# Dilated v projection: its staging for DRAM in the raw weights' ring instead of the score rows' ring

## The chip, the cores and the metric

The kernel runs on one core of one Trainium2 chip. The metric is the device time of one execution in microseconds; the runs shown of the kernel before took 1883.52 us in the median (1883.05 to 1884.08, three runs).

## What is computed

One layer of a decoder trunk over 1024 tokens of width 1024, all in float32. The part that matters here is the dilated window attention, one of four token mixers:

```python
DIL_PATTERNS = ((128, 1), (512, 4), (2048, 16))      # (window, dilation) of three groups
qb, kb, vb = (a.reshape(bsz, seq, N_DIL_GROUPS, N_DIL_HEADS, HEAD_DIM) for a in (qb, kb, vb))
...
for g, (window, dil) in enumerate(DIL_PATTERNS):
    idx = t_idx[:, None] - dil * jnp.arange(window // dil + 1)[None, :]
    kg, vg = jnp.take(k[:, :, g], idx, axis=1), jnp.take(v[:, :, g], idx, axis=1)
    s = jnp.einsum('bqhd,bqnhd->bhqn', q_blk[:, :, g], kg) * HEAD_DIM ** -0.5
    s = s - slopes[g][:, None, None] * dists                 # then softmax over n
    outs.append(jnp.einsum('bhqn,bqnhd->bqhd', p, vg))
```

q, k and v of every mixer are columns of one product, RMSNorm(x) @ w_in. After the mixers come gated branch projections, an output projection and a squared-ReLU MLP.

## The kernel before

Every float32 product is made of float32r parts: an operand is split into a high part and a low rest, and three matmuls on TensorE stand for one (`mm3`, L148 to L155: high times high, high times low, low times high). Weights come through three rings of four buffers each (`wpiece`, L117): a piece of 256 KB is loaded by SP's queue into `wr` (L125), GpSimd makes its high part `wh` (L132) and its low part `wl` (L133), and with that `wr` is free again. The buffers of `wr` have other tenants too: the copies `gs` of gate logits on their way to DRAM (L492 to L495) use the same ring.

The mixers run as twelve units, two (`pr` 0 and 1, two heads each) for each of six groups. A unit has a projection part, `p_`, and an attention part, `a_`; the projection of the next unit is written ahead of the end of this one's attention, so that its matmuls (`lin`, `linv`, in three PSUM banks of the pool `ps_lin`) fill TensorE while attention waits for VectorE and ScalarE. For a dilated group the order of work is: v of the group (`proj_v`), q and k of its first pair (`proj_pair`, whose `lin_T` takes 128 columns of weights in two pieces), attention of the first pair, q and k of the second, attention of the second.

`proj_v` makes v in four blocks of two token tiles (48 matmuls of 256 columns each, `linv`). For dilation 4 and 8 (the reference's 16, in 8 residue classes) tokens have to be regrouped by residue, which goes through DRAM: ScalarE copies each half of the bank to a staging tile `vs` (high part, L158), VectorE writes the low rest beside it (L162), ScalarE's queue stores the half to `v_d` (L390), and when all is stored, SP's queue loads it back in the new order into `v` (L399): 8 loads for dilation 4, 16 for dilation 8. Staging in the kernel before takes one tile of the ring `s` for both halves. That ring has five buffers (`NS`, L56) and holds the score rows of attention (`s2` in `attend_dil`) and the rows of the differential mixer's norm (`ysq`, `sp`, `r0`, L671 to L694).

What stands in which order on an engine is set by a list scheduler: it takes instructions by priority (the order in the code, with the evacuations put ahead by `EVAC_LEAD`) as their inputs and buffers come free in its own model of time. A ring with no free buffer thus moves instructions to later places in the queues; on the chip each engine and each queue goes through its own list in order.

Of the kernel before, what the change touches and what calls it, by code (L numbers as in the profile page):

```python
# [12 lines left out]
F32 = mybir.dt.float32  # L13
F32R = mybir.dt.float32r
# [8 lines left out]
P = 128  # L23
T = 1024
# [35 lines left out]
NWR, NWH, NS, NPT, NQK = 4, 4, 5, 6, 12  # L60
# [4 lines left out]
def kernel(  # L65
# [27 lines left out]
    wp = ctx.enter_context(tc.tile_pool(name="wp", bufs=1))  # L93
# [19 lines left out]
    def nm(s):  # L113
        uid[0] += 1
        return f"{s}_{uid[0]}"
# [33 lines left out]
    def mm3(ps, pairs):  # L149

        n = len(pairs)
        for i, ((ah, al), (bh, bl)) in enumerate(pairs):
            nc.tensor.matmul(ps, ah, bh, start=(i == 0), stop=False, skip_group_check=True)  # L153
            nc.tensor.matmul(ps, ah, bl, start=False, stop=False, skip_group_check=True)  # L154
            nc.tensor.matmul(ps, al, bh, start=False, stop=(i == n - 1), skip_group_check=True)  # L155

    def evac_hi(o, i, scale=1.0):
        nc.scalar.activation(o, i, AF.Copy, scale=scale)  # L158

    def evac_lo(o, i, hi, scale=1.0):  # L160
        if scale == 1.0:
            nc.vector.tensor_sub(o, i, hi.bitcast(F32))  # L162
        else:
            nc.vector.scalar_tensor_tensor(o, i, scale, hi.bitcast(F32), op0=ALU.mult, op1=ALU.subtract)
# [49 lines left out]
    with ExitStack() as actx:  # L214
# [87 lines left out]
        def w_next(off, n):  # L302
            assert plan[0] == (off, n), (plan[0], off, n)
            plan.pop(0)
            return held.pop() if held else wcols(w_in, off, n)
# [55 lines left out]
        def proj_v(voff, dil, fl=None):  # L361

            n = 260 if fl is not None else 256
            ws = w_next(voff, n)
            vt = [ap_.tile([P, NT, 2, P], F32R, tag="v", bufs=3, name=nm("v")) for _ in range(2)]
            v_d = [dram.tile([T, 4 * 64], F32, name=nm("v_d")) for _ in range(2)] if dil > 1 else None
            per = 1 if fl is not None else 2
            for b0 in range(0, NT, per):
                ps = ps_lin.tile([P, 512], F32, tag="lin", name=nm("linv"))
                for j in range(per):  # L370
                    ts_ = slice((b0 + j) * P, (b0 + j + 1) * P)
                    pairs = [((hTh[:, k, ts_], hTl[:, k, ts_]), ws[k]) for k in range(NK)]
                    if fl is not None:
                        mm3(ps[:, :n], pairs)
                    else:

                        mm3(ps.rearrange("p (a b c) -> p a b c", a=2, b=2)[:, :, j], pairs)
                if dil > 1:
                    vs = s_tile("vs")[:, :T].bitcast(F32R).rearrange("p (a b d) -> p a b d", a=2, d=P)
                with tc.high_priority(offset=EVAC_LEAD):  # L380
                    for p in range(2):
                        i = ps[:, p * per * P:(p + 1) * per * P].rearrange("p (a d) -> p a d", d=64)
                        if dil > 1:
                            o = vs[:, p]
                        else:
                            o = vt[p].rearrange("p b h d -> p (b h) d")[:, 2 * b0:2 * (b0 + per)]
                        evac_hi(o[:, :, 0:64], i)
                        evac_lo(o[:, :, 64:128], i, o[:, :, 0:64])
                        if dil > 1:
                            nc.scalar.dma_start(  # L390
                                v_d[p][b0 * P:(b0 + per) * P, :].rearrange("(b p) c -> p b c", p=P),
                                o.rearrange("p (b h) d -> p b (h d)", b=per).bitcast(F32))
                    if fl is not None:
                        nc.vector.tensor_add(fl[:, :, b0], ps[:, 256:260], bf_row)
            if dil > 1:
                m = T // dil // P
                for p in range(2):
                    for r in range(dil):
                        nc.sync.dma_start(  # L399
                            vt[p][:, r * m:(r + 1) * m].rearrange("p b h d -> p b (h d)").bitcast(F32),  # L400
                            v_d[p].rearrange("(b p r) c -> r p b c", r=dil, p=P)[r])
            return vt

        def s_tile(n):
            return ap_.tile([P, T + 8], F32, tag="s", bufs=NS, name=nm(n))
# [398 lines left out]
        def unit_diff(pr):  # L804
            def p_():
                if pr == 0:
                    state["v"] = proj_v(DIF_V, 1)
                v = state["v"]
                qs, ks = proj_diff(pr)
                return lambda: attend_diff(pr, qs, ks, v[pr])  # L810
            return p_

        def unit_dil(g, pr):
            def p_():
                if pr == 0:
                    state["v"] = proj_v(DIL_V + g * 256, DILATION[g])
                    state["mnl"] = small.tile([P, 2, 4, NT], F32, tag="mnl", bufs=2, name=nm("mnl"))
                v, mnl = state["v"], state["mnl"]
                q, k, kl = proj_pair(DIL_Q + g * 256 + pr * P, DIL_K + g * 256 + pr * P, -0.125, DILATION[g])

                def a_():
                    attend_dil(g, pr, q, k, kl, v[pr], mnl)
                    if pr == 1:
                        dil_stats(g, mnl)
                return a_
            return p_

        def unit_fox(pr):
            def p_():
                if pr == 0:  # L830
                    fl = small.tile([P, 4, NT], F32, name="fl")
                    state["v"] = proj_v(FOX_V, 1, fl)
                    state["cq"] = fox_cum(fl)
                v, cq = state["v"], state["cq"]
                q, k, kl = proj_pair(FOX_Q + pr * P, FOX_K + pr * P, -0.125, 1)
                return lambda: attend_fox(pr, q, k, kl, v[pr], cq)
            return p_
# [602 lines left out]
```

## Time and profile before

| | |
|---|---|
| median of the runs shown | 1883.52 us |
| the profiled execution | 1883.11 us, its span 1881.4 us |
| TensorE busy | 1834.4 us, 98% of the span |
| VectorE, ScalarE, GpSimd busy | 1083.7, 846.2, 766.5 us |
| `vs` evacuations of dilation 4 | from 432.2 us on |
| `vs` evacuations of dilation 8 | last at 549.7 us |

Times in the trace count from the start of the span; the profiled execution has 1.7 us outside it. Matmuls overlap in the pipeline, so that a row's own length is more than its share: what a matmul costs is the distance from one start to the next.

### The profile page before, as it was taken

To read this page: it belongs to the slowest core of one execution; us is meant where nothing else is said; L and a number is where in the kernel's file an instruction comes from. 1 tells how busy PE (TensorE), PEld (TensorE's weight loads), DVE (VectorE), ACT (ScalarE), POOL (GpSimd) and SP (SyncE) were. 2 spreads that over 40 slices of the span, in tenths; PEclk is the share of its full clock that TensorE was granted. 3 is DMA by queue.
4 is the path that set the end of the run, shared out by engine and by line. 5 is a ranking of instruction groups with operands and counts; after the bars stand their busy time and mean duration, and the time that the engine had idled before them with its cause. 6 is when DMAs were issued, how large, how long until landed. Compare 5 with 4: busy or idle time off the path is not lost.

```text
span 1881.4 us, 27436 instructions
## 1 busy us (share of the span) xinstructions
PE 1834.4 (98%) x9683; PEld 1554.3 (83%) x9683; DVE 1083.7 (58%) x1907; ACT 846.2 (45%) x1731; POOL 766.5 (41%) x715
## 2 busy tenths in 40 slices
PE   7999999999999999998999999989999999999998
PEld 7888888889888889887788879978888888888886
DVE  5144464544454555677653596595444445759677
ACT  4133334454464544454342454554554545444344
POOL 5434244423222243532323471077564641418165
PEclk9999999999989999999999999999999999999999
DMA  4634213234243221126314764525444448675455
GB/s 147 160 103 118 68 51 90 62 102 157 68 139 92 63 79 57 54 63 188 98 59 149 250 225 158 174 90 183 158 141 160 136 146 305 220 229 198 123 179 185
DMA packets 214137, 255.39 MB, mean 136 GB/s; under 512 B 17392, under 2 KB 136560, under 8 KB 214000
## 3 DMA queue, kind: packets, MB, share of 16 engines
q1 hardware_dynamic: 174880, 176.39, 30.8%
q10 hardware_dynamic: 39120, 77.25, 12.2%
q8 instruction: 76, 1.25, 0.3%
q14 instruction: 61, 0.50, 0.1%
HBM read 174.25 MB, written 65.70 MB: 128 GB/s over the span
## 4 chain that ended last, share of the span: by engine, by line
PE 88%; DVE 5%; DMA 2%; POOL 2%; ACT 1%; issue 1%; SPq 1%; ACTq 0%; POOLq 0%; DVEq 0%
PE pu L1145 5%; PE pu L1146 5%; PE pu L1143 5%; PE lg L153 5%; PE pd L1334 5%; PE pd L1332 5%; PE lg L154 5%; PE pd L1333 5%; PE lg L155 5%; PE lin L153 5%; PE lin L154 5%; PE lin L155 5%; PE pt L430 3%; PE linv L154 2%; PE linv L153 2%; PE linv L155 2%
## 5 line engine op out<-in xcount | busy, mean ns | idle before, releaser
L132 POOL TENSOR_SCALAR wh<-wr 128x512 fp32r<-128x512 f32 (+1 forms) x156 | 106.4, 683 | 438.6 <-PE linv L155 116.9
L133 POOL TENSOR_TENSOR wl<-wr,wh 128x512 fp32r<-128x512 f32 (+1 forms) x160 | 220.1, 1379 | 9.5
L153 PE MATMUL lg<-hTh,wh 128*128 128x512 f32 x464 | 185.7, 400 | 0.0
L154 PE MATMUL lg<-hTl,wh 128*128 128x512 f32 x464 | 185.6, 400 | 0.0
L155 PE MATMUL lg<-hTh,wl 128*128 128x512 f32 x464 | 184.9, 399 | 0.0
L1333 PE MATMUL pd<-wl,sh 128*128 128x512 f32 x444 | 174.3, 393 | 0.6 <-DVE wl L1054 0.6
L1334 PE MATMUL pd<-wh,sl 128*128 128x512 f32 x444 | 173.9, 394 | 0.0
L1332 PE MATMUL pd<-wh,sh 128*128 128x512 f32 x444 | 171.9, 394 | 0.0
L153 PE MATMUL lin<-hTh,wh 128*128 128x512 f32 x384 | 153.1, 399 | 0.0
L154 PE MATMUL lin<-hTl,wh 128*128 128x512 f32 x384 | 153.0, 399 | 0.0
L155 PE MATMUL lin<-hTh,wl 128*128 128x512 f32 x384 | 151.9, 398 | 0.0
L1054 DVE TENSOR_TENSOR sl<-mg,sh 128x512 fp32r<-128x512 f32 x111 | 107.0, 967 | 69.9 <-ACT sh L1053 69.7
L1053 ACT CAST sh<-mg 128x512 fp32r<-128x512 f32 x111 | 68.6, 620 | 142.5 <-PE pd L1333 126.8
L435 DVE TENSOR_TENSOR ptl<-pt,pth 128x512 fp32r<-128x512 f32 (+2 forms) x168 | 99.3, 605 | 55.5 <-ACT pth L434 54.2
L434 ACT CAST pth<-pt 128x512 fp32r<-128x512 f32 (+2 forms) x168 | 84.7, 524 | 95.4 <-PE pt L430 91.1
L153 PE MATMUL linv<-wh,hTh 128*128 128x256 f32 (+1 forms) x384 | 112.0, 293 | 2.2 <-ACT hTh L195 0.9
L154 PE MATMUL linv<-wl,hTh 128*128 128x256 f32 (+1 forms) x384 | 112.0, 292 | 0.0
L155 PE MATMUL linv<-wh,hTl 128*128 128x256 f32 (+1 forms) x384 | 111.9, 292 | 0.0
L153 PEld LDWEIGHTS lg<-hTh,wh 128*128 128x128 f32 x464 | 87.9, 189 | 17.9 <-DVE dst L162 0.2
L155 PEld LDWEIGHTS lg<-hTh,wl 128*128 128x128 f32 x464 | 87.6, 189 | 17.3
L154 PEld LDWEIGHTS lg<-hTl,wh 128*128 128x128 f32 x464 | 87.8, 189 | 17.1
L1333 PEld LDWEIGHTS pd<-wl,sh 128*128 128x128 f32 x444 | 83.4, 188 | 20.6 <-DVE wl L1054 1.0
(360 smaller groups left out, 5044.8 us busy)
## 6 DMA issues: line engine op xcount, KB each, us to landing
wr<-in_w_in_dram SPq DMA_DIRECT2D x132, 256.0 KB
br<-in_w_down_dram SPq DMA_DIRECT2D x96, 256.0 KB
mg<-sa_s SPq DMA_DIRECT2D x64, 256.0 KB
gl<-gs ACTq DMA_DIRECT2D x58, 256.0 KB
sg<-gl SPq DMA_DIRECT2D x58, 256.0 KB
mg<-sa_a SPq DMA_DIRECT2D x48, 256.0 KB
wr<-in_w_out_dram SPq DMA_DIRECT2D x36, 256.0 KB
dm<-dst ACTq DMA_DIRECT2D x64, 128.0 KB
```

The costliest lines, as they stand in the source:

```text
L132: nc.gpsimd.tensor_scalar(hi, raw, 1.0, 1.0, op0=ALU.mult, op1=ALU.mult)
L133: (eng or nc.gpsimd).tensor_sub(lo, raw, hi.bitcast(F32))
L153: nc.tensor.matmul(ps, ah, bh, start=(i == 0), stop=False, skip_group_check=True)
L154: nc.tensor.matmul(ps, ah, bl, start=False, stop=False, skip_group_check=True)
L155: nc.tensor.matmul(ps, al, bh, start=False, stop=(i == n - 1), skip_group_check=True)
L435: nc.vector.tensor_sub(lo[:, :n], ps[:, :n], hi[:, :n].bitcast(F32))
L1054: nc.vector.tensor_sub(o[1], i, o[0].bitcast(F32))
L1143: nc.tensor.matmul(ps[:, cs], w_, bh[:, k, cs], start=first and k == 0, stop=False, skip_group_check=True)
L1145: nc.tensor.matmul(ps[:, cs], w_, bl[:, k, cs], start=False, stop=False, skip_group_check=True)
L1332: nc.tensor.matmul(ps, sh[0][:, ts_], w[0], start=start and j == 0, stop=False, skip_group_check=True)
L1333: nc.tensor.matmul(ps, sh[0][:, ts_], w[1], start=False, stop=False, skip_group_check=True)
L1334: nc.tensor.matmul(ps, sh[1][:, ts_], w[0], start=False, stop=last and j == NPAIR - 1, skip_group_check=True)
```

## The change

The staging tile of both halves, one buffer of the ring `s`, is replaced by two buffers of the ring `wr`, one for each half:

```diff
                 if dil > 1:
-                    vs = s_tile("vs")[:, :T].bitcast(F32R).rearrange("p (a b d) -> p a b d", a=2, d=P)
+
+                    vs = [wp.tile([P, 520], F32, tag="wr", bufs=NWR, name=nm("vs"))[:, :512].bitcast(F32R)
+                          .rearrange("p (b d) -> p b d", d=P) for _ in range(2)]
...
                         if dil > 1:
-                            o = vs[:, p]
+                            o = vs[p]
```

The instructions are the same; those on which buffers depend come in another order, in the stretch from the v projection of dilation 4 to that of dilation 8. Lines behind the change are higher by two.

SP's queue at the v projection of dilation 4 (`wr` with 128x4x128 are pieces of q and k weights, `v` from `v_d` the regrouped loads). Before:

```order
L125 DMA wr_4669<-in_w_in_dram 128x4x128
L125 DMA wr_4675<-in_w_in_dram 128x4x128
L125 DMA wr_4745<-in_w_in_dram 128x4x128
L125 DMA wr_4751<-in_w_in_dram 128x4x128
L680 DMA ysq_4817<-yd_89 128x512
L125 DMA wr_5046<-in_w_in_dram 128x4x128
L672 DMA ysq_4832<-yd_89 128x512
L125 DMA wr_5052<-in_w_in_dram 128x4x128
L399 DMA v_4430<-v_d_4432 128x2x256 x4
```

After:

```order
L682 DMA ysq_4821<-yd_89 128x512
L125 DMA wr_4673<-in_w_in_dram 128x4x128
L125 DMA wr_4679<-in_w_in_dram 128x4x128
L674 DMA ysq_4836<-yd_89 128x512
L401 DMA v_4430<-v_d_4432 128x2x256 x4
L401 DMA v_4431<-v_d_4433 128x2x256 x4
L125 DMA wr_4749<-in_w_in_dram 128x4x128
L125 DMA wr_4755<-in_w_in_dram 128x4x128
```

The two pieces of q weights (4669 and 4675 before, 4673 and 4679 now) still stand ahead of the v loads, but in buffers that staging tiles of the third block hold before them; the two pieces of k weights (4745 and 4751 before, 4749 and 4755 now) have moved behind all eight v loads.

TensorE at the end of the third block of the v projection of dilation 8 (`sc`, `pt` and `o` are scores, transposes and outputs of the attention of dilation 4, second pair). Before:

```order
L155 MATMUL linv_5566<-wh_5445,hTl 128x2x128
L411 MATMUL sc_5243<-kA_5116,qA_5044 128x128
L412 MATMUL sc_5243<-klA_5118,qA_5044 128x128
L411 MATMUL sc_5248<-kA_5116,qA_5044 128x256
L412 MATMUL sc_5248<-klA_5118,qA_5044 128x256
L430 MATMUL pt_5230<-ident,s_5219 128x128 x3
L411 MATMUL sc_5270<-kA_5116,qA_5044 128x128
```

After:

```order
L155 MATMUL linv_5572<-wh_5449,hTl 128x2x128
L153 MATMUL linv_5629<-wh_5431,hTh 128x2x128
L154 MATMUL linv_5629<-wl_5432,hTh 128x2x128
L155 MATMUL linv_5629<-wh_5431,hTl 128x2x128
L153 MATMUL linv_5629<-wh_5431,hTh 128x2x128
L154 MATMUL linv_5629<-wl_5432,hTh 128x2x128
```

Before, 75 matmuls of attention follow the third block alone and the fourth block (5622) comes behind them; now the fourth block (5629) follows at once, and attention comes between its matmuls and behind it, with the q projection of dilation 8 in its later part.

SP's queue at the v projection of dilation 8. Before, the k weights (5773 and 5779) are loaded long ahead:

```order
L125 DMA wr_5697<-in_w_in_dram 128x4x128
L125 DMA wr_5703<-in_w_in_dram 128x4x128
L125 DMA wr_5773<-in_w_in_dram 128x4x128
L125 DMA wr_5779<-in_w_in_dram 128x4x128
L680 DMA ysq_5194<-yd_89 128x512
```

After:

```order
L125 DMA wr_5705<-in_w_in_dram 128x4x128
L125 DMA wr_5711<-in_w_in_dram 128x4x128
L401 DMA v_5454<-v_d_5456 128x256 x8
L401 DMA v_5455<-v_d_5457 128x256 x8
L125 DMA wr_5781<-in_w_in_dram 128x4x128
```

The k weights (5781) stand behind all sixteen v loads now.

## Rows read from the trace of the kernel before

**Rows 1.** The page: busy time of each engine, its share of the span, and its instructions.

```profile
PE 1834.4 (98%) x9683; PEld 1554.3 (83%) x9683; DVE 1083.7 (58%) x1907; ACT 846.2 (45%) x1731; POOL 766.5 (41%) x715
```

**Rows 2.** Busy time of each engine by stretch (us), then TensorE's granted clock, the DMA engines' busy share and GB/s.

```profile
526.87:533.70 6.83, 6.64 (x32) 6.62 (x33) 4.66 (x21) 4.85 (x18) 0.00 (x0) 0.50 0.10 38
...
540.52:543.93 3.41, 3.41 (x19) 3.41 (x18) 1.41 (x4) 1.04 (x3) 0.00 (x0) 0.50 0.88 291
...
523.77:540.18 16.41, 12.29 (x71) 11.12 (x70) 13.61 (x50) 12.80 (x44) 0.00 (x0) 0.79 0.09 32
...
450.94:462.40 11.46, 11.46 (x50) 9.24 (x50) 6.13 (x8) 6.54 (x9) 10.33 (x10) 1.00 0.80 238
```

**Rows 3.** TensorE in order of time around the fourth v block of dilation 8: start, length, operation; in brackets the idle time before it and what ended that.

```profile
509.79 0.28 PE L155 MATMUL linv<-wh,hTl 128*128 128x256 f32 x1
...
523.49 0.28 PE L155 MATMUL linv<-wh,hTl 128*128 128x256 f32 x1
524.84 0.33 PE L411 MATMUL sc<-kA,qA 128*128 128x128 f32 x1 [1.06 <-DVE mnl L725]
...
537.09 0.28 PE L412 MATMUL sc<-klB,qB 128*128 128x256 f32 x1
539.22 0.35 PE L439 MATMUL o<-pth,v 128*128 128x256 f32 x1 [1.85 <-DVE y L454]
...
549.28 0.28 PE L441 MATMUL o<-ptl,v 128*128 128x256 f32 x1
...
550.13 0.45 PE L682 MATMUL rms<-sp,ones_blk 128*128 128x512 f32 x1
...
550.65 0.42 PE L155 MATMUL lin<-hTh,wl 128*128 128x512 f32 x1
...
557.64 0.40 PE L154 MATMUL lin<-hTl,wh 128*128 128x512 f32 x1
...
560.90 0.39 PE L153 MATMUL lin<-hTh,wh 128*128 128x512 f32 x1
```

**Rows 4.** All instructions on the tile `vs`: shortest, median and longest (ns), first and last start (us).

```profile
L158 ACT ACTIVATE vs<-linv x16: 361/383/389, 432.2 to 549.7; 128x256 fp32r<-128x256 f32 x16
L162 DVE TENSOR_TENSOR vs<-linv,vs x16: 399/424/425, 433.4 to 550.1; 128x256 fp32r<-128x256 f32 x16
L390 ACTq DMA_DIRECT2D v_d<-vs x16: 366/366/545, 433.8 to 551.0; - x16
```

**Rows 5.** ScalarE in order of time, in the attention of dilation 4, second pair: first and last softmax rows, and the staging between.

```profile
524.81 0.40 ACT L727 ACTIVATE s<-s,mnl 128x128 f32<-128x128 f32 x1 [0.52 <-DVE mnl L725]
...
536.21 0.36 ACT L158 ACTIVATE vs<-linv 128x256 fp32r<-128x256 f32 x1
...
538.66 0.65 ACT L158 ACTIVATE vs<-linv 128x256 fp32r<-128x256 f32 x2
539.19 0.51 ACT L727 ACTIVATE s<-s,mnl 128x256 f32<-128x256 f32 x1
```

**Rows 6.** ScalarE's queue and SP's queue in order of time: a store of a gate copy out of a `wr` buffer, and the load that waits for that buffer; then loads of a `wr` piece on SP and the splits on GpSimd that wait for them.

```profile
399.79 0.33 ACTq L495 DMA_DIRECT2D gl<-gs  x1
...
401.84 0.37 SPq L125 DMA_DIRECT2D wr<-in_w_in_dram  x1
...
985.90 0.37 SPq L125 DMA_DIRECT2D wr<-in_w_in_dram  x1
...
988.90 1.05 POOL L132 TENSOR_SCALAR wh<-wr 128x512 fp32r<-128x512 f32 x1 [6.28 <-DMA wr<-in_w_in_dram]
...
79.25 0.37 SPq L125 DMA_DIRECT2D wr<-in_w_in_dram  x1
...
84.33 0.62 POOL L132 TENSOR_SCALAR wh<-wr 128x512 fp32r<-128x512 f32 x1 [0.18 <-DMA wr<-in_w_in_dram]
```

**Rows 7.** ScalarE in order of time at the third and fourth v block of dilation 4.

```profile
445.33 0.38 ACT L158 ACTIVATE vs<-linv 128x256 fp32r<-128x256 f32 x1 [2.11 <-PE linv L155]
446.21 0.37 ACTq L390 DMA_DIRECT2D v_d<-vs  x1
...
451.85 0.37 ACTq L390 DMA_DIRECT2D v_d<-vs  x1
...
453.13 0.37 ACTq L390 DMA_DIRECT2D v_d<-vs  x1
```

**Rows 8.** SP's queue in order of time at the v loads of dilation 4, and at those of dilation 8 (for a merged row the length of the whole).

```profile
455.84 2.75 SPq L399 DMA_DIRECT2D v<-v_d  x4
...
459.20 2.42 SPq L399 DMA_DIRECT2D v<-v_d  x4
...
553.20 8.56 SPq L399 DMA_DIRECT2D v<-v_d  x16
```

**Rows 9.** GpSimd in order of time: the splits of the first pieces of q weights, dilation 4.

```profile
450.19 1.29 POOL L133 TENSOR_TENSOR wl<-wr,wh 128x512 fp32r<-128x512 f32 x1
451.45 0.62 POOL L132 TENSOR_SCALAR wh<-wr 128x512 fp32r<-128x512 f32 x1
```

**Rows 10.** TensorE in order of time: end of the v projection of dilation 4, start of the q projection, start of the k projection.

```profile
451.25 0.40 PE L153 MATMUL lin<-hTh,wh 128*128 128x512 f32 x1
...
462.40 0.39 PE L153 MATMUL lin<-hTh,wh 128*128 128x512 f32 x1
...
462.86 0.40 PE L155 MATMUL lin<-hTh,wl 128*128 128x512 f32 x1
```

## Prediction

> **What bounds the kernel now.** I read the page first: TensorE is busy 1834.4 of 1881.4 us, 98%, and no other engine is over 58% [rows 1]. A change that adds or removes no instruction can pay only where TensorE waits, or works at the lower clock. So I went by stretches next. The diff touches the v projections of dilation 4 and 8, and at the second of them lies one of the few places of the program where TensorE is starved: from 523.77 to 540.18 it is busy 12.29 of 16.41 us, and in 526.87 to 533.70 and again in 540.52 to 543.93 it was granted 0.50 of its clock, that is 1.2 in place of 2.4 GHz [rows 2]. The timeline shows why [rows 3, 5]. The first v block of dilation 8 has its last matmul at 509.79, yet it is evacuated into `vs` only from 536.21 on. Staging needs a buffer of the score rows' ring, which attention holds. Three blocks fill the three PSUM banks of `ps_lin`, so from 523.49 the fourth block cannot start, and attention has TensorE to itself, waiting for VectorE (1.06 us idle before its first score, 1.85 us before an output at 539.22).
>
> How much is lost there: the order shows 75 attention matmuls in that stretch. Where such matmuls run densely, eight of them take 0.85 us, 549.28 to 550.13 [rows 3], or 0.106 each; 75 are 8.0 us. So 16.4 - 8.0 = 8.4 us are lost, and in 540.52 to 543.93, where block four runs at half clock, half of 3.41, or 1.7. About 10.1 us can be won at most.
>
> **The change: the gain at dilation 8.** Staging now takes `wr` buffers, which are free once GpSimd has split the weights, so the evacuations come right behind each block. Block four follows block three at once, and part of it and of the q projection stands between attention's matmuls. Attention itself is paced by ScalarE and VectorE, and staging is now in its way there. An evacuation costs 0.383 us on ScalarE, 0.424 on VectorE, and 0.366 for the store's issue in ScalarE's queue [rows 4]. Block two's two halves come ahead of the first softmax: 2 x (0.38 + 0.37) = 1.5 us later. Blocks three and four come inside: four copies and four issues, 3.0 us, against three copies and two issues, 1.9 us, that the stretch from 524.81 to 539.70 holds today [rows 5]: 1.1 more. So the last score, which ends at 537.37 today [rows 3], ends at about 540.0. Four matmuls of the q projection and seven of attention stand just ahead of it in the new order (0.9 + 0.7 us); I let half fit into the wait, 540.8.
>
> From there TensorE has 44 matmuls of the q projection left and 14 of attention before the k projection. Fourteen of the first kind take 3.26 us (557.64 to 560.90) [rows 3], 0.233 each: 10.3 + 1.5 = 11.8, so the k projection starts at 552.6. Today it starts at 560.90. But outputs that ran from 549.28 to 550.13, and norm matmuls from there to 550.65, now come behind it: 1.4 us are only put off. The gain is 560.9 - 552.6 - 1.4 = **6.9 us**. Its bounds: 4.3 if attention slips by twice what I add (2.6 us more), 9.5 if staging slows nothing (2.6 less). I keep the middle, since copies and issues are counted from rows.
>
> **What it costs at dilation 4.** Here the staging of today is in no one's way: TensorE has no idle time from 450.94 to 462.40 [rows 2], because q and k weights lie in `wr` long before. Now the first q piece needs a buffer that block three's first half holds until it is stored. Block three is copied at 445.33 and stored at 446.21 [rows 7]. A store out of the same ring issued at 399.79 let the next load go at 401.84 [rows 6]: 2.05 us. So that load is issued at 448.3. From load to split the rows have 3.0 us (985.90 to 988.90) where little else moves and 5.1 (79.25 to 84.33) where the queue is full [rows 6]; here the queue is empty, so 3.0: 451.3. The split takes 0.62 and the low part 1.29 [rows 9]: high part 452.0, low part 453.3. TensorE wants the first at 451.25 [rows 10] and, four matmuls on, the second: 0.75 + 0.35 = **1.1 us** of waiting (2.6 if the load takes 1.5 longer).
>
> The k weights are the worse part. Their loads stand behind all eight v loads on SP. Those wait for the last stores, issued at 451.85 and 453.13 [rows 7]; with 2.05 us each, four loads go from 453.9 and four more end at 453.9 + 2.75 + 2.42 = 459.1 by today's issue times [rows 8]. Load to split again takes 3.0 to 5.1: 462.1 to 464.2. TensorE, 1.1 us late, wants the first k piece at 463.5. At the lower end only the low part is late, by 0.1; at the upper end the high part is there at 464.9 (1.4 of waiting) and the low part at 466.2, 0.8 after the two matmuls that can go first: **2.2 us**. I take the upper end: the eight loads move 2 MB in the same queue just ahead, in a stretch where the DMA engines are 80% busy at 238 GB/s today [rows 2]. Second pieces follow 2.3 us of matmuls later and are hidden by those.
>
> At dilation 8 the q pieces have all of attention as cover. The k pieces stand behind sixteen v loads, which take 8.56 us to issue [rows 8]. Half of them can go when the first half of block four is stored, and the k projection starts at 552.6: with the first stores done at about 537 the issue ends near 546, a split 5.1 later near 551. Hidden, with 1 us to spare.
>
> **Sum.** -6.9 + 1.1 + 2.2 = -3.6 us. The profiled execution took 1883.1, 0.4 below the median of the runs: 1879.5 on its scale, **1879.9** on the median's. Behind 600 us the order is unchanged, and TensorE's list moves as a whole.
>
> **Rivals.** (1) *The k weights of dilation 4 come in time* (lower end): -6.9 + 1.1 + 0.1 = -5.7, 1877.8. For it: fewer weight loads compete there than today. Against: 2 MB at today's 238 GB/s take 8.8 us, which puts the split past 463. The Trainium skill, "DMA: Bandwidth & Descriptors", section "Anatomy of one DMA", gives a transfer about 2 us fixed and 436 GB/s beyond that; by it, as an estimate, eight loads and the piece behind them would be down near 461.5, and the sum would be this rival's. The trace's 238 GB/s at 80% busy speaks against that rate.
>
> (2) *The clock falls at dilation 4.* About 2.2 us of idle time near 465, behind a dense stretch, could do what the waits before 526.87 did: a granted clock of 0.50 [rows 2]. Priced by the shorter such stretch, 3.41 us at half rate, in dense matmuls: 1.7 more, sum -1.9, 1881.6. For it: both low stretches of rows 2 follow idle time. Against: the wait is split in two by matmuls, and the stretch from 450.94 to 462.40 ahead of it is at 1.00 without idle time. The Trainium skill, "TensorE: Matmul & The Clock Gate", Part 1, says that the throttled state is the default and activity releases it. By that rule this rival is what a long enough wait does; both halves of rows 2 agree.
>
> (3) *Slower: SP's queue holds up the k weights at both places.* The mechanism is that of the 2.2 us, further out: `wr` loads land only when the v loads ahead are through. Each microsecond beyond my landing times (464.2; and 551 plus the 1 to spare) is one for TensorE. It is a draw from 3.6 us in all, and slower by over 0.2% if both loads are some 4 us later than I have them: -3.6 + 2 x 3.9 = +4.2, 1887.7. For it: nothing is left to run on TensorE in between, as its list is in order. Against: 5.1 us is already the slow end of the rows.
>
> That the change does not do what it says is excluded: the order shows block four behind block three, and the k loads behind the v loads.
>
> **How the numbers follow.** Forecast 0.5, (1) 0.2, (2) 0.2, (3) 0.1. A measurement of this kernel tells about 0.2%, 3.8 us, from no change, so the bound is 1879.75. The forecast stands at that bound, and with the 2.6 us either way of its gain almost half of it lies below; with most of (1), faster is 0.44. Of (3) most, and a little of the rest, is slower: 0.07. Within: 0.49. The range takes in (1), the forecast and (2), and leaves out (3) and the far ends: 1877.0 to 1884.0.
>
> **What would show it.** Right: `vs` copies of dilation 8 from about 510; TensorE busier than 12.29 in 16.4 us behind the third block, with no stretch at 0.50 there; a wait of TensorE for GpSimd's splits (L132, L133) of about 1 us at the start of q and 2 at the start of k, dilation 4. Wrong: waits for splits at dilation 8; a fall of the clock near 465; or attention slipping so that TensorE is idle over 5 us between block four and the q projection.

## The result, and the profile after

The changed kernel takes **1885.66 us** in the median of 20 runs (1883.24 to 1889.50), the kernel before 1882.93 in 20 (1878.45 to 1885.78): a ratio of 1.0017, 95% interval 1.001 to 1.0023, or 1.9 to 4.3 us slower. I had forecast 1879.9, 3.6 us faster. The profiled execution took 1885.47 us, its span 1883.7.

The stretches that answer to [rows 2], in the changed kernel: busy time of PE, PEld, DVE, ACT and POOL, then TensorE's granted clock, the DMA engines' share and GB/s.

```profile
450.94:462.40 11.46, 10.31 (x48) 7.96 (x47) 4.71 (x8) 6.43 (x9) 3.78 (x4) 1.00 0.81 250
465.38:468.08 2.70, 0.00 (x1) 0.00 (x0) 1.38 (x2) 1.18 (x2) 0.62 (x1) 0.90 1.14 319
467.55:474.38 6.83, 6.16 (x14) 4.42 (x15) 0.53 (x1) 0.00 (x0) 6.63 (x8) 0.50 0.49 114
523.77:540.18 16.41, 16.41 (x140) 16.30 (x139) 9.00 (x25) 10.53 (x23) 0.00 (x0) 1.00 0.32 113
546.06:549.47 3.41, 3.41 (x15) 3.02 (x14) 1.31 (x7) 2.14 (x10) 0.32 (x1) 0.50 0.81 248
```

The fourth line is the forecast gain: where TensorE was busy 12.29 of 16.41 us at 0.79 of its clock, it is now busy throughout at 1.00. The second and third are the loss: 2.70 us with no matmul at all, and behind them 6.83 us at half clock, where before there was neither. The fifth is what is left at dilation 8: 3.41 us at half clock behind a wait of 0.94. TensorE in order of time, for the places of [rows 3, 10]:

```profile
451.91 0.40 PE L684 MATMUL rms<-sp,ones_blk 128*128 128x512 f32 x1
...
453.54 0.50 PE L153 MATMUL lin<-hTh,wh 128*128 128x512 f32 x1 [0.99 <-POOL wh L132]
...
454.90 0.51 PE L155 MATMUL lin<-hTh,wl 128*128 128x512 f32 x1 [0.16 <-POOL wl L133]
...
465.00 0.39 PE L155 MATMUL lin<-hTh,wl 128*128 128x512 f32 x1
468.08 0.79 PE L153 MATMUL lin<-hTh,wh 128*128 128x512 f32 x1 [2.70 <-POOL wh L132]
...
476.90 0.39 PE L153 MATMUL lin<-hTh,wh 128*128 128x512 f32 x1
...
562.23 0.39 PE L153 MATMUL lin<-hTh,wh 128*128 128x512 f32 x1
...
580.37 0.39 PE L153 MATMUL lin<-hTh,wh 128*128 128x512 f32 x1
```

The same matmuls in the kernel before, where [rows 3, 10] have no line for them:

```profile
450.78 0.40 PE L682 MATMUL rms<-sp,ones_blk 128*128 128x512 f32 x1
...
462.18 0.39 PE L155 MATMUL lin<-hTh,wl 128*128 128x512 f32 x1
...
467.99 0.39 PE L153 MATMUL lin<-hTh,wh 128*128 128x512 f32 x1
...
577.63 0.39 PE L153 MATMUL lin<-hTh,wh 128*128 128x512 f32 x1
```

I read the loss by how late the same matmul is against the first trace of before. The norm matmul behind the v projection of dilation 4 is 1.13 us late (451.91 for 450.78): nothing of that is the change, it comes from one stretch at half clock near 239 us, ahead of it. The q projection adds 1.7 (its last matmul starts at 465.00 for 462.18, 2.82 late). The k projection starts 5.68 late (468.08 for [rows 10]'s 462.40), 2.86 more. Its 24 matmuls to the second half take 8.82 us (to 476.90) where they took 5.59 (462.40 to 467.99), 3.23 more: the half clock. Together 7.8 us. At dilation 8 the k projection starts at 562.23 for 560.90, only 1.33 late: 7.6 us were won. From 580 on, the lateness is 2.74 (580.37 for 577.63), since 1.4 us of outputs and norm matmuls came behind the k projection. The gain that stays is 6.2, and the balance of this pair of traces over the stretch is 2.74 - 1.13 = +1.6 us.

Why the weights are late: SP's queue (with GpSimd's splits and ScalarE's stores below it), which answers to [rows 7 to 9].

```profile
449.55 1.75 SPq L125 DMA_DIRECT2D wr<-in_w_in_dram  x2
451.39 0.46 SPq L674 DMA_DIRECT2D ysq<-yd  x1
455.95 5.17 SPq L401 DMA_DIRECT2D v<-v_d  x8
461.23 8.55 SPq L125 DMA_DIRECT2D wr<-in_w_in_dram  x5
...
544.84 8.93 SPq L401 DMA_DIRECT2D v<-v_d  x16
553.88 0.93 SPq L125 DMA_DIRECT2D wr<-in_w_in_dram  x2
```

```profile
452.87 0.62 POOL L132 TENSOR_SCALAR wh<-wr 128x512 fp32r<-128x512 f32 x1 [31.47 <-PE rms L685]
...
467.41 0.62 POOL L132 TENSOR_SCALAR wh<-wr 128x512 fp32r<-128x512 f32 x1 [10.60 <-DMA wr<-in_w_in_dram]
...
558.28 0.62 POOL L132 TENSOR_SCALAR wh<-wr 128x512 fp32r<-128x512 f32 x1 [11.90 <-PE pt L432]
```

```profile
447.34 0.37 ACTq L392 DMA_DIRECT2D v_d<-vs  x1
...
452.99 0.37 ACTq L392 DMA_DIRECT2D v_d<-vs  x1
```

The q load goes 2.2 us after the store out of its buffer (447.34 to 449.55) and is split 3.3 later. (The bracket of that split names a norm matmul that ended just before; in e4, below, the same split starts at 452.91 and its bracket names the load.) The v loads go at 455.95, 2.96 after the store of the fourth block's first half. The first k piece is issued behind all eight, at 461.23, and its split starts 6.2 us later; before 467.41 GpSimd stood idle for 10.60 us, waiting for that load. At dilation 8 the same order costs nothing: the first k piece is split at 558.28 and wanted at 562.23.

### The profile page after: what moved, and what is told of

It reads as the page before. It is cut to its first block, busy times and chain, and to the rows that moved or that the text cites. A ratio compares the mean times of both kernels' runs of the same rounds, so it can differ in the third digit from the quotient of the medians.

```text
span 1883.7 us, 27440 instructions
## 1 busy us (share of the span) xinstructions
PE 1835.2 (97%) x9683; PEld 1553.1 (82%) x9683; DVE 1071.3 (57%) x1907; ACT 846.3 (45%) x1731; POOL 768.2 (41%) x715
## 4 chain that ended last, share of the span: by engine, by line
PE 87%; DVE 5%; DMA 3%; issue 1%; ACT 1%; POOL 1%; SPq 1%; ACTq 0%; POOLq 0%; DVEq 0%
PE pd L1336 5%; PE pd L1334 5%; PE pd L1335 5%; PE pu L1147 5%; PE pu L1148 5%; PE pu L1145 5%; PE lg L153 5%; PE lg L154 5%; PE lg L155 5%; PE lin L153 5%; PE lin L155 5%; PE lin L154 5%; PE pt L432 3%; PE linv L154 2%; PE linv L155 2%; PE linv L153 2%
## 5 line engine op out<-in xcount | busy, mean ns | idle before, releaser
L154 PEld LDWEIGHTS lg<-hTl,wh 128*128 128x128 f32 x464 | 87.9, 189 | 17.1
```

## The experiments

Six kernels took the two halves of the change, the queue, the idle time and the buffers apart; two further traces of before and one of after show what repeats.

**e1, staging in `wr` at dilation 8 alone; e2, at dilation 4 alone.** With these, the order at one dilation is that of the changed kernel and at the other that of before.

```diff
-                    vs = [wp.tile(... tag="wr" ...) for _ in range(2)]
+                    if dil == 8:      # e2: dil == 4
+                        vs = [wp.tile(... tag="wr" ...) for _ in range(2)]
+                    else:
+                        vs = s_tile("vs")[:, :T]....; vs = [vs[:, 0], vs[:, 1]]
```

> Staging in the raw weights' ring at dilation 8 alone; dilation 4 stages in the score rows' ring as before, and the order around 450 to 480 us is that of the kernel before. Theory (the loss sits at dilation 4, the gain at dilation 8 is kept to the end): TensorE has no wait for GpSimd's splits at q and k of dilation 4 and no stretch at 0.50 near 468; the k projection of dilation 8 starts some 7.6 us earlier than before, 1.4 of that is put off, and about 6.2 us remain at 600 and at the end: ratio to the kernel before 0.9967 (0.9960 to 0.9975). Rival A (what is won at dilation 8 is given back behind 600 us): 6 us ahead at 600, but ratio 0.999 to 1.000.

> Staging in the raw weights' ring at dilation 4 alone. Theory: q waits 1.2 to 1.6 us, k waits 2.7 to 2.9, then 6.8 us at half clock cost 3.2; nothing behind takes it back, since the waits of attention at dilation 8 are set by ScalarE and VectorE and move as a whole: +7.7 us, ratio 1.0041 (1.003 to 1.005). Rival B (the delay is partly taken up by later waits of TensorE, so that dilation 8 in the changed kernel won less than it seems): ratio 1.001 to 1.002.

Measured: e1 0.9973 (0.9964 to 0.9982), e2 1.0046 (1.0033 to 1.0058). The two effects, -0.0027 and +0.0046, add up to +0.0019, the changed kernel's +0.0017. So rivals A and B fall by the ratios: the gain of one half is kept to the end, and the loss of the other is not taken up as a whole. (In e2's trace the loss at dilation 4 is 8.5 us by the lateness of the same matmul, with a k wait of 4.1; the waits at dilation 8 stay, but no half clock follows them there, which makes that stretch 3.4 us shorter than in the first trace of before.) In e1 TensorE has no idle time at dilation 4 (first line); at dilation 8 a rest of the old trouble is left (second line).

```profile
450.94:475.00 24.06, 24.06 (x110) 19.69 (x110) 10.26 (x14) 10.10 (x15) 15.56 (x16) 1.00 0.64 197
529.00:545.00 16.00, 13.87 (x88) 12.43 (x87) 10.69 (x40) 11.16 (x39) 3.76 (x4) 0.89 0.65 194
```

In e2, TensorE's waits from 450 to 476 (total, times, longest), and the stretch behind the longest:

```profile
PE lin L153 <- POOL wh L132: 5.1, 2, 4.1
PE lin L155 <- POOL wl L133: 0.2, 1, 0.2
```

```profile
467.64:474.46 6.82, 4.54 (x10) 3.14 (x11) 0.69 (x1) 0.05 (x1) 5.26 (x6) 0.50 0.42 114
```

**e3, the changed kernel with the v loads of dilation 4 written behind q and k.** Nothing but SP's order changes (and, by it, one pair of GpSimd's instructions).

```diff
-            if dil > 1:
+            def v_load():
                 ... nc.sync.dma_start(vt[p]..., v_d[p]...)
...
                 q, k, kl = proj_pair(...)
+                if pr == 0 and DILATION[g] == 4:
+                    state["v_load"]()
```

> The changed kernel, with the eight v loads of dilation 4 written behind the q and k projections: the first k piece stands ahead of all v loads in SP's queue, the second behind three of them; all buffers are as in the changed kernel. Theory (place in SP's queue makes the k wait): first k piece issued near 456 and split near 460, no wait at the k projection, no stretch at 0.50 near 468; the q wait of 1.2 to 1.6 stays. 6.1 us less than the changed kernel: ratio to the kernel before 0.9983 to 0.9990 by the interval of the changed kernel (1.001 to 1.0023 less 0.0032). Rival C (buffers or the DMA engines, not the place, set the landing): k still waits 2 us or more, ratio as the changed kernel, 1.001 to 1.0023. Rival D: the v loads land later and attention's first output waits instead: a wait of TensorE for v behind the k projection, ratio 1.000 to 1.0015.

Measured: 0.9993 (0.9984 to 1.0001), 0.0024 under the changed kernel; expected was 0.0032, so the ratio lies just outside the range that I gave. SP's queue and the splits:

```profile
454.60 0.37 SPq L127 DMA_DIRECT2D wr<-in_w_in_dram  x1
455.02 1.52 SPq L403 DMA_DIRECT2D v<-v_d  x3
456.65 0.40 SPq L127 DMA_DIRECT2D wr<-in_w_in_dram  x1
457.10 3.22 SPq L403 DMA_DIRECT2D v<-v_d  x5
```

```profile
457.63 0.62 POOL L134 TENSOR_SCALAR wh<-wr 128x512 fp32r<-128x512 f32 x1 [2.09 <-DMA wr<-in_w_in_dram]
...
462.39 0.62 POOL L134 TENSOR_SCALAR wh<-wr 128x512 fp32r<-128x512 f32 x1 [2.72 <-DMA wr<-in_w_in_dram]
```

```profile
463.93 0.39 PE L155 MATMUL lin<-hTh,wh 128*128 128x512 f32 x1
```

Its stretch at half clock at dilation 8:

```profile
537.52:544.35 6.83, 6.24 (x26) 5.88 (x27) 3.36 (x16) 3.46 (x14) 1.21 (x1) 0.50 0.69 209
```

The first piece goes at 454.60 and is split 3.0 us later; the second, behind three v loads, takes 5.7. The k projection starts at 463.93 without a wait, and from there to 475 the clock is 1.00; the q wait stays, 1.1 and 0.2. The place in the queue made the k wait; rival C falls. No wait for v came in its place at the start of attention, so D falls too. By lateness this trace saves the whole 6.1 us at dilation 4 (k wait and half clock); at dilation 8 it gains 4.4 for the 6.2 of the changed kernel, since 6.83 us at half clock follow a wait of 1.90 there (last fence), where the changed kernel has 3.41. That accounts for what the ratio lacks.

**e4, twelve matmuls to fill the wait.** The changed kernel with 12 added matmuls, their result unused, between the q and the k projection of dilation 4:

```diff
+            if dil == 4 and qoff == DIL_Q + 256:
+                fl_ = ps_t.tile([P, 512], F32, tag="t", name=nm("fill"))
+                for i in range(12):
+                    nc.tensor.matmul(fl_, last[7][0], hTh[:, 1, :512], start=(i == 0), stop=(i == 11), ...)
             lin_T(koff, ev_k)
```

> The changed kernel with 12 added matmuls of 512 columns (results unused) on TensorE between the q and the k projection of dilation 4, 0.23 us each, 2.8 us in all, where the changed kernel waits 2.7. SP's order shifts a little (the first k piece behind four v loads). Theory (the clock falls because TensorE stood idle): the k projection starts as late as in the changed kernel, within 0.5 us, but no stretch at 0.50 lies between 465 and 480, and its 24 first matmuls take 5.75 us in place of 8.99: 3.2 us less than the changed kernel, ratio to the kernel before 0.9993 to 1.0006. Rival E (the clock falls for another reason there, such as the dense work ahead or the DMA load): 0.50 near 468 all the same, ratio 1.001 to 1.0025.

Measured: 0.9997 (0.9988 to 1.0006), 0.0020 under the changed kernel, though it does more work. TensorE in order of time, and the stretch that was at half clock:

```profile
465.31 2.95 PE L362 MATMUL fill<-hTh,wh 128*128 128x512 f32 x12
468.10 0.39 PE L153 MATMUL lin<-hTh,wh 128*128 128x512 f32 x1
```

```profile
467.55:474.38 6.83, 6.83 (x31) 5.50 (x30) 0.62 (x1) 0.49 (x1) 6.47 (x8) 1.00 0.39 98
```

The split of the first k piece:

```profile
463.39 0.62 POOL L132 TENSOR_SCALAR wh<-wr 128x512 fp32r<-128x512 f32 x1 [6.51 <-DMA wr<-in_w_in_dram]
464.10 1.29 POOL L133 TENSOR_TENSOR wl<-wr,wh 128x512 fp32r<-128x512 f32 x1
```

The k projection starts at 468.10, as late as in the changed kernel (468.08), and runs at 1.00: its first 24 matmuls take 5.59 us for 8.82. So at this place it is the idle time that brings the clock down, and rival E falls. What e4 does not show is that such work is free. In its shifted SP order the first k piece is split by 465.39, when the q projection ends, so that without the twelve matmuls there would hardly have been a wait: they hold the k projection back by 2.8 us themselves. (TensorE's order around dilation 8 shifts too, so the ratio is less clean than the rows.)

**e5, e6, the fourth block kept out of `wr`.** Both stage the first three blocks in `wr` and the fourth in the score rows' ring; e5 at dilation 8 alone (dilation 4 as before), e6 at both.

```diff
+                    if b0 < 6:        # e5: dil == 8 and b0 < 6
                         vs = [wp.tile(... tag="wr" ...) for _ in range(2)]
+                    else:
+                        vs = s_tile("vs")...
```

> As e1_only8 (dilation 4 as before), but at dilation 8 only the first three blocks are staged in the raw weights' ring and the fourth in the score rows' ring. The q and k weights of dilation 8 then take the buffers of blocks two and three, and are loaded ahead of the v loads; q and k matmuls come earlier in TensorE's order, between attention's. Theory (at dilation 8 what is left after e1 is TensorE waiting behind q weights that wait for the fourth block's buffers): the wait of 1.9 us near 538 and the stretch at 0.50 near 540 of e1 go, 1.9 + 1.7 us: ratio to the kernel before 0.9973 - 0.0019 = 0.9954 (0.9945 to 0.9965). Rival F (attention's own pace, VectorE and ScalarE, sets the end of that stretch, whatever stands between): ratio as e1, 0.9965 to 0.998, with waits for mnl or pt of the same sum. Rival G (the sixteen v loads now stand behind ten weight loads in SP's queue): attention of dilation 8 waits for v, ratio over 0.998.

> The changed kernel with the fourth block of both dilations staged in the score rows' ring and the first three in the raw weights' ring. Theory (the loss at dilation 4 is nothing but q and k weights waiting for the buffers of blocks three and four): no wait for splits at q and k of dilation 4, no stretch at 0.50 near 468, ratio as e5, 0.9945 to 0.9965. Rival H (two more tenants in the ring cost something in any case, by the v loads or the stores in the same stretch): the q wait or a part of it stays, ratio over e5 by 0.001 or more.

Measured: e5 0.9961 (0.9949 to 0.9974), e6 0.9956 (0.9942 to 0.9970). The stretch around the fourth block of dilation 8 in e5 (first fence), and in e6 the q and k projections of dilation 4 and then that stretch (second):

```profile
523.77:560.00 36.23, 36.23 (x219) 31.68 (x218) 20.93 (x61) 19.17 (x55) 15.23 (x17) 1.00 0.49 139
```

```profile
445.00:475.00 30.00, 30.00 (x160) 25.62 (x159) 11.99 (x16) 11.07 (x18) 16.24 (x17) 1.00 0.78 244
523.77:560.00 36.23, 36.23 (x223) 31.97 (x223) 21.24 (x60) 20.03 (x56) 14.89 (x16) 1.00 0.51 142
```

No idle time and no half clock is left at either place. So the loss at dilation 4 is not staging in `wr` as such, but what the fourth block's staging there does: it leaves the q weights the third block's buffers and the k weights its own. H falls. At dilation 8 the weights come early enough for q and k matmuls to stand between attention's, and the waits of e1 go: F and G fall by the rows. By the ratios e5 is below e1 by 0.0012, but the intervals overlap. By lateness both e5 and e6 win 9.9 us at dilation 8 against the first trace of before, and e6 loses nothing at dilation 4. e6 has the lowest ratio of all, clear of before and of the changed kernel, though not of e5.

**e7, e8, e9, the same kernels again.** Before a second and a third time, after a second time.

> The kernel before once more, for a second trace. Theory: the low clock of the stretch around the fourth v block of dilation 8 belongs to the order, so that it shows again: at least one stretch at 0.50 between 523 and 545, and the waits of 3 us in all. If it is chance, the granted clock is 1.00 there, and the gain of the changed kernel at dilation 8 would be some 3.4 us less. The fall at 238.86, which the changed kernel's trace has and the first trace of before has not, comes ahead of all changes: chance, so either may show.

> The changed kernel once more, for a second trace. Theory (each wait at dilation 4 brings the clock down): the waits of 1.2 us at q and 2.7 us at k again, a stretch at 0.50 from about 467 on again, 3.2 us (or 1.7 if it is the shorter kind). If the fall is chance, as that near 239 us is, the clock is 1.00 there and the loss at dilation 4 is 4.5 in place of 7.7.

> The kernel before a third time. Its first trace shows 10.2 us at half clock in 523 to 545, its second 3.4, with the same waits. Theory (waits in the same places, clock by chance of where they fall): 3.4 to 10.2 us again, so that the gain of the changed kernel at dilation 8 is 3.6 to 6.2 us by the execution it is set against. If the first trace was typical, 10.2 again.

The stretch around the fourth block of dilation 8 in before: the first trace, then e7, then e9.

```profile
523.77:545.00 21.23, 17.11 (x98) 15.94 (x97) 15.34 (x54) 13.85 (x47) 0.00 (x0) 0.76 0.23 76
```

```profile
523.77:545.00 21.23, 17.05 (x120) 15.41 (x119) 16.57 (x55) 15.74 (x51) 0.11 (x1) 0.92 0.25 86
```

```profile
523.77:545.00 21.23, 17.06 (x119) 15.27 (x118) 16.41 (x55) 15.89 (x51) 0.00 (x0) 0.92 0.26 90
```

TensorE is busy for the same 17.1 us, but gets through 98 matmuls in the first trace and 120 and 119 in the others: 10.2 us at half clock there, 3.4 in each of these. By the lateness of the same matmul, both come out of the stretch 2.6 us earlier than the first. So the trace from which I predicted was the slow one of three in this stretch. Its whole time was not unusual: 1883.11 us, against a median of 1882.93, with e7 and e9 at 1881.54 and 1881.89. And by its ratio e1 is 5.1 us (3.4 to 6.8) faster than before in the median, while its trace gains 5.3 on the first trace in this stretch and 2.7 on e7 and e9; which of them is the usual case stays open. In after, the second time, the waits and the fall at dilation 4 are there again (5.5 us gained at dilation 8, +2.7 in balance by the same reading as above):

```profile
PE lin L153 <- POOL wh L132: 4.0, 2, 2.9
PE lin L155 <- POOL wl L133: 0.2, 1, 0.2
```

```profile
468.21:475.03 6.82, 6.52 (x15) 4.64 (x16) 0.00 (x0) 0.00 (x0) 6.62 (x8) 0.50 0.43 104
```

The fall near 239 us, ahead of every change, is in both traces of after and in e7 and e9, but not in the first of before or in e3 and e5: chance, worth some 1.3 to 1.5 us of any one trace.

## Why the prediction was wrong

The mechanisms were the ones named. What failed is the sum. The fall of the clock behind the k wait stood in it at nothing, left to a rival, and cost 3.2 us. The gain at dilation 8 was priced from a single trace of before, the slow one of three there. And the two waits at dilation 4 came to 4.6 us for my 3.3.

- **The clock at dilation 4 (failed, the largest).** The forecast had TensorE wait at k and go on at full speed. The clock fell to 0.50 in both traces of after, for 6.83 and 6.82 us, which I had named as a sign of being wrong. I made that rival (2), with 0.2, and priced it by the shorter stretch of [rows 2], 1.7; it cost 3.2. My arguments against it were none: the dense stretch at 1.00 ahead of the wait did not keep the clock up, and the wait came in one piece of 2.70 us, not split in two. e4 shows that what counts here is whether the wait is idle. The rows for the right reading were there, since both half-clock stretches of [rows 2] follow idle time. The Trainium skill, "TensorE: Matmul & The Clock Gate", Part 1, has the throttled state as the default that activity releases; e4, where work took the place of the idle time and the clock stayed at 1.00, agrees.
- **The gain at dilation 8 (mechanism right, size off).** The evacuations come right behind the blocks, the fourth block follows the third, and the k projection starts 7.6 us earlier with 1.4 put off: 6.2 for my 6.9, inside my bounds. But that is against the first trace. Some 2.6 us of it are half clock that this one execution lost; against e7 and e9 the gain is 6.2 - 2.6 = 3.6, and 5.5 - 2.6 = 2.9 by the second trace of after. I took the 10.1 us that were lost there as a property of the kernel; the waits are one (17.1 busy of 21.2 three times), the low clock behind them only in part.
- **The k wait at dilation 4 (right, somewhat small).** 2.86 for 2.2, and 2.9 idle in the second trace. By the common delay of 1.13, the v loads went at 454.8 (I had 453.9: the last stores took 2.96, not 2.05), the k piece at 460.1 (459.1), and from load to split took 6.2, over what I called the slow end, 5.1. The upper end was the right one to take, and it was no upper end. The estimate beside rival (1), a landing near 461.5, was off by nearly 5 us: all nine transfers of 256 KB needed 455.95 to 467.41, other traffic beside them. The Trainium skill, "DMA: Bandwidth & Descriptors", section "Anatomy of one DMA", gives that fit for one DMA that GpSimd issues; these go by SP's queue, one behind another.
- **The q wait (right in kind, somewhat small).** 1.7 for 1.1: load 2.2 after the store for 2.05, split 3.3 after the load for 3.0, and small losses at each restart.
- **Dilation 8's k weights (right).** Hidden, with more to spare (4 us) than the 1 that I gave. So rival (3), my only slower case, was not what happened: it needed both places late. The slower outcome came from the clock at one, and from a smaller gain.
- **The sum.** With the measured terms of the first pair of traces, -6.2 + 1.7 + 2.86 + 3.2 = +1.6. With 3.6 for the gain it is +4.2, and the means of two traces after (+1.6, +2.7) and three before (0, -2.6, -2.6) differ by 3.9; the runs' interval is 1.9 to 4.3. So the median lay above my range's end of 1884.0, by 1.7. How often before falls into its slow variant of that stretch is not known from three traces.

## What to carry to other kernels

A wait of TensorE in a dense stretch can cost its length and then as much again in half clock. The k wait did so in all three traces that have it (after, e8, e2): 2.70, 2.92 and 4.07 us idle, and 3.2, 3.4 and 2.5 us more for the 24 matmuls behind. The q waits of 1.0 to 1.5 us, in five traces, brought no fall. Nor does each wait of some 2 us: ahead of the product `pb`, which starts between 1084 and 1100 us and which none of these changes touch, TensorE waits 1.8 to 2.5 us in all eleven traces, and half clock follows in four. So price a new wait of 2 or 3 us with the fall included, as the likelier case, and a wait that is there already by more than one trace. When staging borrows buffers from a ring of loads, ask which load gets each buffer next and what stands ahead of it in its queue; here three blocks in that ring were free of cost and the fourth cost all.

## What the runs showed of the hardware that I had not expected

- With twelve added matmuls, 2.8 us of useless work, in place of 2.70 us of idle time, a half-clock stretch of 6.83 us did not come (e4).
- The same order with the same waits ran 10.2 us at half clock in one execution, and 3.4 in two others; by the lateness behind it that was 2.6 us.
- A weight load that is split 3.0 us after its issue with no load of v ahead of it (e3) takes 6.2 behind eight of them, and as long behind four (e4, 457.24 to 463.39).
